# Compressed keys' products placed behind the first branch's second output products, and kept down-projection weights split one k-tile later, in a one-core decoder layer

## The chip, the cores and the metric

The kernel runs on one core of one Trainium2 chip. The metric is the device time of one execution in microseconds (us). TensorE (PE) does the matrix products, VectorE (DVE) and ScalarE (ACT) the element-wise work, GpSimd (POOL) a few small steps, and SyncE (SP) issues nearly all DMA transfers.

## The reference

One layer of a decoder on 256 positions with 2048 channels, in float32. Three token mixers share one input projection; a gated sum of their outputs goes through `w_o`, and a feed-forward block follows.

```
h = rms_norm(x);  p = h @ w_in
y_a = conformer_conv(...)            # GLU, causal conv of 31 taps, LayerNorm, silu, @ w_a_out
y_b = chunked_spatial_gating(...)    # gelu, LayerNorm, 128x128 mixing, @ w_b_out
y_c = native_sparse_attention(...)   # compressed, selected and window branch, @ w_c_out
x = x + rms_norm((g_a*y_a + g_b*y_b + g_c*y_c) @ w_o)
u = causal_depthwise_conv(rms_norm(x) @ w_up)
x = x + rms_norm((silu(u_g) * u_v) @ w_down)
```

The compressed branch joins 32 neighbouring positions of keys (and of values) to one block: `hid = silu(einsum(blocks + pe, w1))`, and `hid @ w2` gives the compressed key. These are the products that the first part of the change moves. The second part is in `@ w_down`.

## The kernel before

Float32 operands are multiplied as two reduced-precision parts. Every weight tile of 128 x 1024 is fetched by SP into a ring of five (`wraw`), ACT writes its high part (`whi`), DVE the rest (`wlo`), and PE takes three products (high by high, high by rest, rest by high; lines 194 to 197, 924 to 930). High and rest parts have rings of four tiles each, so a tile can only be split when PE is done with the tile four before it. One such matmul of 512 columns belongs to every line 195, 196, 197 or 929 in the profile.

**The middle of the kernel.** `branch(0, ...)` and `branch(1, ...)` (line 993) compute the gate of the gMLP and of the convolution branch (tiles `pg`) and their output products (tiles `py`), for four blocks of 512 channels each (`cb` 0 to 3). A gate block is 96 matmuls over 8 weight tiles, an output block 48 matmuls over 4 tiles in two halves (`q` 0 and 1). Between these, background work is issued from a queue of generators, `bg`. `pump(ns)` (line 91) adds a budget to `debt` and runs the generator at the head of the queue until the costs that it yields have used the budget up; a branch calls it with `BUDGET = BG` after the first three quarters of a gate block, behind the gate, between the two halves of an output block and behind it. `until(name)` empties the queue up to a mark.

In the queue stand, in this order when the branches begin: the rest of the convolution (`conv_gen`), its LayerNorm (`lna_gen`: mean product `lnpm`, squares, variance product `lnpv` on PE, `lnvar`, reciprocal root, and then eight rounds of normalization, tanh and conversion to `At`, lines 511 to 522), the spatial gating that is left, `cmp_prep(0)` (line 592: 16 additions of `pe` on DVE at line 601, four conversions `bk` on ACT and DVE at lines 605 and 606), `cmp_gen(0)` (line 609: four weight tiles `w1` split through the same rings, 32 products `zp`, two short products `hp` and `kcp`), the same two for the values, the compressed attention `cmp_attn` (line 705: scores `sc`, softmax `ce`, transposes `pcp` copied to `pct`), and the attention units (line 855). The text of the program gives only the order of issue and the dependencies; the framework's scheduler then fixes one order of instructions on each engine, and an engine does its instructions strictly in that order.

**The end.** The down-projection runs twice, over the first and the last 1024 channels: `first = Pair(0)`, `second = Pair(1)` (lines 1468 and 1478). Each has 24 plain k-tiles (`plain`, 12 matmuls, one weight tile) and ten pairs of k-tiles done with seven products in place of eight (`quad`, lines 939 to 959: 21 matmuls, two weight tiles `wraw` and `qa`, and on DVE four additions of 512 columns, three splits of 1024 and one of 512). In the second run the last six plain k-tiles are "kept": their weights are split ahead and multiplied only at the end, one 128 x 512 block of the result after the other, so that the closing norm of a block lies beside the products of the next (lines 1506 to 1526). Four of the six split tiles lie in space that the activations `gh` and `gl` have left, two in the rings. All splits of this part are issued in an order written by hand on ACT and DVE (`fixed`, line 888).

Of the kernel before, what the change touches and what calls it, by code (L numbers as in the profile page):

```python
# [24 lines left out]
R = mybir.dt.float32r  # L25
# [6 lines left out]
T = 256  # L32
# [6 lines left out]
PLAIN = [*range(22, 33), 21, 10, *range(33, NFT)]  # L39

NG, REST = 3, list(range(6, KT))
BA, BB, BC, BG = 2100, 2200, 2200, 5000
PR = 1000
NW0, _ = 9, 6
S1, S2, S3 = 6, 12, 14
# [11 lines left out]
def block(ctx: ExitStack, tc: tile.TileContext, x, xf, fp, cst, rows, sgw, w1, w2, wf_a, wt_bv, wf_bu, wf_c,  # L57
# [8 lines left out]
    marks = set()  # L66
# [21 lines left out]
    bg = deque()  # L88
# [296 lines left out]
    for k in range(KT):  # L385
        for j, cb in ((k, 0), (k, 1)) if k < 14 else ((14, 0), (15, 0)) if k == 15 else ():
            hi, lo = parts[j]
            c = slice(cb * 512, cb * 512 + 512)
# [203 lines left out]
    def cmp_prep(kv):  # L592
        bk = s8([128, 16, 2, 64], R, f"bk{kv}")
        bk_box[kv] = bk
        pe = fps[:, (C_PK, C_PV)[kv]:(C_PK, C_PV)[kv] + 16]
        for c in range(4):
            tmp = q1(f"bt{kv}{c}", (128, 4, 4, 16))
            G.memset(tmp[:, :, :, 15], 0.0)
            for i in range(4):
                jj = 4 * c + i  # L600
                V.tensor_scalar(tmp[:, i, :, 0:15], kd_t[:, kv, :, 2 * jj:2 * jj + 225:16], pe[:, jj:jj + 1], None,
                                op0=ALU.add)
                yield 150
            tf = tmp.rearrange("p i g n -> p i (g n)")
            S.activation(bk[:, 4 * c:4 * c + 4, 0], tf, AF.Copy)
            V.tensor_sub(bk[:, 4 * c:4 * c + 4, 1], tf, bk[:, 4 * c:4 * c + 4, 0].bitcast(F32))
            yield 350

    def cmp_gen(kv):
        bk = bk_box[kv]  # L610
        zp = bank([128, 2, 256], f"zp{kv}")
        for q in range(4):
            hi, lo = piece(w1[kv, :, q * 1024:q * 1024 + 1024], 1024)
            for i in range(4):
                jj = 4 * q + i
                st = bk[:, jj].rearrange("p a n -> p (a n)")
                PE.matmul(zp[:, 0], lhsT=st, rhs=hi[:, i * 256:i * 256 + 256], start=(jj == 0), stop=(jj == 15),
                          skip_group_check=True)
                PE.matmul(zp[:, 1], lhsT=st, rhs=lo[:, i * 256:i * 256 + 256], start=False, stop=(jj == 15),
                          skip_group_check=True)  # L620
            yield 1300
        zs = [q1(f"zs{kv}{a}") for a in range(2)]
        for a in range(2):
            S.activation(zs[a], zp[:, a], AF.Copy)
        hp = bank([128, 2, 64], f"hp{kv}")
        for h in range(2):
            for a in range(2):
                PE.matmul(hp[:, h], lhsT=zs[a][:, h * 128:h * 128 + 128], rhs=sel, start=(a == 0), stop=(a == 1))
        w2s = q1(f"w2s{kv}", (128, 2, 128))
        nc.sync.dma_start(w2s, w2[:, kv])  # L630
        hid = P1.tile([128, 2, 64], F32, tag="hid", bufs=2, name=f"hid{kv}")
        for h in range(2):
            th = P1.tile([128, 64], F32, tag="hth", bufs=2, name=f"hth{kv}{h}")
            S.activation(th, hp[:, h], AF.Tanh, scale=0.5)
            V.scalar_tensor_tensor(hid[:, h], th, 1.0, hp[:, h], op0=ALU.add, op1=ALU.mult)
            yield 200
        if kv == 0:
            ps = bank([128, 64], "kcp")
            for h in range(2):
                PE.matmul(ps, lhsT=w2s[:, h], rhs=hid[:, h],  # L640
                          start=(h == 0), stop=(h == 1))
            V.tensor_mul(kcb.rearrange("p g n -> p (g n)"), ps, cs[:, K_KM:K_KM + 64])
            yield 200
        else:
            hr = [q1(f"hidr{h}", (128, 2, 128)) for h in range(2)]
            for h in range(2):
                for gg in range(2):
                    V.tensor_copy(hr[h][:, gg].rearrange("p (j m) -> p j m", j=4),
                                  hid[:, h, gg * 32:gg * 32 + 32][:, None, :].to_broadcast([128, 4, 32]))
            yield 800  # L650
            for gg in range(2):
                ps = bank([128, 128], f"vcp{gg}")
                for h in range(2):
                    PE.matmul(ps, lhsT=hr[h][:, gg], rhs=w2s[:, h], start=(h == 0), stop=(h == 1))
                for j in range(4):
                    V.scalar_tensor_tensor(vbd[:, gg, j], ps, cs[:, K_RJ + j:K_RJ + j + 1], cs[:, K_BM:K_BM + 128],
                                           op0=ALU.mult, op1=ALU.mult)
                    yield 270

    sel = P1.tile([128, 64], F32, name="sel")  # L660
    with tc.issue_after(fetched[0]):
        V.tensor_add(sel, idn[:, 0:64], idn[:, 64:128])
    for kv in range(2):
        bg.append(cmp_prep(kv))
        bg.append(cmp_gen(kv))

    kkv = s8([128, 2, 1024], F32, "kkv")
# [325 lines left out]
    def branch(bi, act_of):  # L993

        for cb in range(4):
            pg = [PS.tile([128, 512], F32, tag="acc", name=f"pg{bi}{cb}{t}") for t in range(2)]
            for q in range(4):
                hs = granule(wt_g[(bi * 4 + cb) * 4 + q])
                for k in range(4 * q, 4 * q + 4):
                    hi, lo = hs[(k % 4) // 2]  # L1000
                    c = slice((k % 2) * 512, (k % 2) * 512 + 512)
                    for t in range(2):
                        ts = slice(t * 128, t * 128 + 128)
                        mm_t(pg[t], hT[:, k, 0, ts], hT[:, k, 1, ts], hi[:, c], lo[:, c], k == 0, k == KT - 1)
                if q < 3:
                    pump(BUDGET)
            tgs = {}
            for t in range(2):
                for a in range(2):
                    tgs[t, a] = q1(f"mg{bi}{cb}{t}{a}")  # L1010
                    with tc.high_priority(offset=int(PR)):
                        gated[0] = S.activation(tgs[t, a], pg[t][:, a * 256:a * 256 + 256], AF.Tanh,
                                                scale=rh[:, t:t + 1]).ins
            marks.add("gates")
            pump(BUDGET)
            py = [PS.tile([128, 512], F32, tag="acc", name=f"py{bi}{cb}{t}") for t in range(2)]
            for q in range(2):
                hs = granule(wt_p[(bi * 4 + cb) * 2 + q])
                if cb == 0 and q == 0:
                    until("BA"[bi])  # L1020
                act = act_of()
                for k in range(4 * q, 4 * q + 4):
                    hi, lo = hs[(k % 4) // 2]
                    c = slice((k % 2) * 512, (k % 2) * 512 + 512)
                    for t in range(2):
                        ts = slice(t * 128, t * 128 + 128)
                        pe_last[0] = mm_t(py[t], act[:, k, 0, ts], act[:, k, 1, ts], hi[:, c], lo[:, c], k == 0, k == 7)
                if q == 0:
                    pump(BUDGET)
            for t in range(2):  # L1030
                for a in range(2):
                    cc = slice(cb * 512 + a * 256, cb * 512 + a * 256 + 256)
                    y = mac[:, t, cc] if bi == 0 else tgs[t, a]
                    with tc.high_priority(offset=int(PR)):
                        V.scalar_tensor_tensor(y, tgs[t, a], 1.0, py[t][:, a * 256:a * 256 + 256], op0=ALU.add,
                                               op1=ALU.mult)
                        if bi:
                            V.tensor_add(mac[:, t, cc], mac[:, t, cc], y)
            pump(BUDGET)
# [436 lines left out]
        first.plain(i)  # L1476
    first.combine()
    second = Pair(1)
    kept = []
    i = 0  # L1480
    for j in range(NQ):
        while i < (3, 5, 7, 9, 10, 12, 14, 15, 17, 18)[j]:
            second.plain(i)
            if i == 2:
                for t in range(2):
                    for n in range(2):
                        first.result(t, n, fixed)
            i += 1
        second.quad(j)
        for x in range(0 if j < NQ - 5 else 1 if j < NQ - 1 else KEEP - 4):  # L1490
            k = NP - KEEP + len(kept)
            into = None
            if j < NQ - 1:
                kt = P2.tile([128, 11, T], R, tag=("gh", "gl")[j % 2], bufs=4, name=f"kept{k}")
                into = kt[:, 0:8].rearrange("p (a b) c -> p a (b c)", a=2)
            kept.append((PLAIN[k], weights(wt_dn[1, k], into)))
    assert i == NP - KEEP and len(kept) == KEEP
    nc.sync.dma_start(gain[:, 1024:2048], row(3072, 1024))
    back = s16(P0, [128, 2, D], F32, "back")
# [150 lines left out]
```

## Time and profile before

| | |
|---|---|
| time, median of 3 runs | 1594.03 us (1593.75 to 1594.13) |
| the profiled execution's own time | 1593.3 us |
| its span in the profile | 1591.5 us |
| mean granted TensorE clock | 0.993 |
| PE, DVE, ACT busy | 1559.4, 1291.6, 912.7 us |
| DMA | 193 GB/s mean |

The span is the time from the first to the last recorded instruction. A row of a timeline reads: start in us from the span's start, duration, engine, line of the kernel, operation, output <- inputs, number of instructions merged; in brackets the idle time of the engine before it and what ended it. A row of the view by windows gives for one stretch the busy time and number of instructions of PE, of PE's weight loads, DVE, ACT and POOL, then the granted TensorE clock (1.00 is full speed), the DMA share and GB/s.

### The profile page before, as it was taken

The numbers are of one execution on the slowest core, as the hardware profiler recorded it, in microseconds if no ns is written. First come the engines' busy times: TensorE is split into PE (matmuls) and PEld (weight loads), VectorE is DVE, ScalarE is ACT, GpSimd is POOL, SyncE is SP. The second block draws the span as 40 slices with busy tenths as digits, with TensorE's granted clock in tenths as the row PEclk, the third lists the DMA queues.
The fourth block names the chain that finished last, engine by engine and source line by source line (L and its number), as shares of the span: only waits on it lengthen the run. The fifth ranks groups of instructions, "written<-read, shape, count | busy, mean of one in ns | idle before, by whom it ended". The sixth has DMA issues, their size and how long they took to land.

```text
span 1591.5 us, 22436 instructions
## 1 busy us (share of the span) xinstructions
PE 1559.4 (98%) x8146; PEld 1323.1 (83%) x8146; DVE 1291.6 (81%) x2210; ACT 912.7 (57%) x1465; POOL 18.2 (1%) x46
## 2 busy tenths in 40 slices
PE   9999999995999999999999999999999999999997
PEld 7888899884887777888888888888888888888876
DVE  8899999778665654878886988888777777789898
ACT  7544544356486665556565765555555555566563
POOL 1000020000000000000000000000000000000000
PEclk9999999997999999999999999999999999999999
DMA  9555556654544445566674665556665656766672
GB/s 374 187 195 183 186 173 212 196 188 134 193 143 145 155 151 187 183 199 199 231 260 158 214 193 189 186 188 193 189 192 188 189 186 191 228 212 215 197 267 92
DMA packets 85440, 307.95 MB, mean 193 GB/s; under 512 B 9808, under 2 KB 10832, under 8 KB 84304
## 3 DMA queue, kind: packets, MB, share of 16 engines
q1 hardware_dynamic: 83952, 301.91, 58.1%
q0 software_dynamic: 944, 4.19, 0.8%
q8 instruction: 64, 1.05, 0.3%
q10 hardware_dynamic: 432, 0.41, 0.1%
q14 instruction: 48, 0.39, 0.1%
HBM read 301.23 MB, written 4.19 MB: 192 GB/s over the span
## 4 chain that ended last, share of the span: by engine, by line
PE 94%; DVE 3%; DMA 1%; ACT 1%; issue 1%; ACTq 0%; DVEq 0%
PE ps L175 29%; PE ps L182 15%; PE pd0b L929 5%; PE pg L195 4%; PE pg L197 4%; PE pg L196 4%; PE pd1a L929 3%; PE py L196 3%; PE py L197 3%; PE py L195 3%; PE poa L929 2%; PE pg1a L929 2%; PE pg0a L929 2%; PE pd0a L929 2%; PE po L195 1%; PE po L197 1%
## 5 line engine op out<-in xcount | busy, mean ns | idle before, releaser
L147 DVE TENSOR_TENSOR wlo<-wraw,whi 128x1024 fp32r<-128x1024 f32 (+1 forms) x376 | 457.4, 1218 | 108.4 <-ACT whi L146 102.0
L146 ACT ACTIVATE whi<-wraw 128x1024 fp32r<-128x1024 f32 (+1 forms) x376 | 393.3, 1052 | 156.4 <-PE pg L197 58.4
L175 PE MATMUL ps<-h2T,whi 128*128 128x512 f32 x1360 | 325.0, 391 | 0.0
L175 PEld LDWEIGHTS ps<-h2T,whi 128*128 128x128 f32 x1360 | 249.8, 188 | 48.2
L182 PEld LDWEIGHTS ps<-h2T,wlo 128*128 128x128 f32 x1360 | 174.5, 191 | 6.7
L182 PE MATMUL ps<-h2T,wlo 128*128 128x256 f32 x1360 | 176.6, 283 | 0.0
L175 PE MATMUL ps<-hT,whi 128*128 128x512 f32 x640 | 157.4, 392 | 0.0
L217 ACT ACTIVATE t<-ps 128x256 f32<-128x256 f32 x125 | 47.6, 382 | 187.0 <-PE ps L175 186.6
L894 DVE TENSOR_TENSOR wlowraw<-wraw,whiwraw 128x1024 fp32r<-128x1024 f32 x90 | 108.6, 1223 | 37.6 <-ACT whiwraw L894 36.1
L175 PEld LDWEIGHTS ps<-hT,whi 128*128 128x128 f32 x640 | 116.0, 188 | 21.3
L894 ACT ACTIVATE whiwraw<-wraw 128x1024 fp32r<-128x1024 f32 x90 | 94.6, 1057 | 48.6 <-PE py L197 17.4
L218 DVE TENSOR_TENSOR t<-ps,t 128x256 f32<-128x256 f32 x125 | 52.6, 422 | 70.3 <-ACT t L217 69.9
L478 DVE SCALAR_TENSOR_TENSOR cv<-hb,fps,cv 128x256 f32<-128x256 f32 x240 | 104.9, 477 | 0.2 <-ACT cv L474 0.2
L196 PE MATMUL pg<-wlo,hT 128*128 128x512 f32 x256 | 100.7, 394 | 0.0
L197 PE MATMUL pg<-whi,hT 128*128 128x512 f32 x256 | 100.7, 393 | 0.0
L195 PE MATMUL pg<-whi,hT 128*128 128x512 f32 x256 | 98.6, 393 | 0.0
L182 PEld LDWEIGHTS ps<-hT,wlo 128*128 128x128 f32 x640 | 84.7, 190 | 4.7
L182 PE MATMUL ps<-hT,wlo 128*128 128x256 f32 x640 | 86.8, 283 | 0.0
L196 PEld LDWEIGHTS pg<-wlo,hT 128*128 128x128 f32 x256 | 48.1, 188 | 10.8 <-issue 1.1
L197 PEld LDWEIGHTS pg<-whi,hT 128*128 128x128 f32 x256 | 48.1, 188 | 10.5 <-issue 0.7
L195 PEld LDWEIGHTS pg<-whi,hT 128*128 128x128 f32 x256 | 47.9, 188 | 10.4 <-issue 0.7
L1379 ACT ACTIVATE fa<-fs,fps 128x256 f32<-128x256 f32 x88 | 52.4, 596 | 1.2 <-DVE fs L220 0.9
(1334 smaller groups left out, 2792.3 us busy)
## 6 DMA issues: line engine op xcount, KB each, us to landing
wraw<-in_wf_up_dram SPq DMA_DIRECT2D x176, 512.0 KB, 4.1
wraw<-in_wt_g_dram SPq DMA_DIRECT2D x64, 512.0 KB, 3.8
wraw<-in_wt_p_dram SPq DMA_DIRECT2D x48, 512.0 KB, 4.3
wraw<-in_wt_dn_dram SPq DMA_DIRECT2D x48, 512.0 KB, 4.4
wraw<-in_wf_a_dram SPq DMA_DIRECT2D x32, 512.0 KB, 3.8
wraw<-in_wt_gp_dram SPq DMA_DIRECT2D x20, 512.0 KB, 4.3
wraw<-in_wt_dq_dram SPq DMA_DIRECT2D x20, 512.0 KB, 5.2
qa<-in_wt_dq_dram SPq DMA_DIRECT2D x20, 512.0 KB, 4.2
```

The costliest lines, as they stand in the source:

```text
L146: S.activation(hi[:, :n], raw[:, :n], AF.Copy)
L147: V.tensor_sub(lo[:, :n], raw[:, :n], hi[:, :n].bitcast(F32))
L175: ins = PE.matmul(ps[:, :, ts], lhsT=ws[k // 8][0][:, c:c + 128], rhs=mov[:, k, :, ts], start=(k == 0 and not t), stop=(k == n - 1), skip_ ...
L182: ins = PE.matmul(ps[:, 1, ts], lhsT=ws[k // 8][1][:, c:c + 128], rhs=mov[:, k, 0, ts], start=False, stop=False, skip_group_check=True).ins
L195: PE.matmul(ps, lhsT=xh, rhs=hi, start=first, stop=False)
L196: PE.matmul(ps, lhsT=xh, rhs=lo, start=False, stop=False)
L197: return PE.matmul(ps, lhsT=xl, rhs=hi, start=False, stop=last).ins
L218: V.tensor_add(t1 if rb is not None else dst, ps[:, 0], t1)
L478: V.scalar_tensor_tensor(ca[:, j], hb[:, j, k:k + T], w(j, k), ca[:, j], op0=ALU.mult, op1=ALU.add)
L894: seq[eng] = [op(*args, **kw).ins]
L929: ins = PE.matmul(bank, lhsT=a[x], rhs=w[y], start=first and j == 0, stop=last and j == 2).ins
L1379: S.activation(a, s, AF.Identity, bias=fps[:, C_FB + f:C_FB + f + 1], scale=w[2])
```

## The change

Three edits in the middle and one at the end:

- A generator `hold("outputs")` is put in the queue between `cmp_prep(0)` and `cmp_gen(0)`. As long as the mark "outputs" is missing it yields 6000 at each step, so that a `pump` gets no further.
- `branch` sets the mark at `cb == 1`, `q == 0`, ahead of the pump between the two halves of the second output block.
- The budget `BG` of a pump in the branches rises from 5000 to 6500.
- In the second run of the down-projection a kept tile is no longer fetched and split directly behind quads 5 to 8 but behind the first plain k-tile that follows each of them; and the space it lies in alternates by the tile's number and no longer by the quad's.

```diff
-BA, BB, BC, BG = 2100, 2200, 2200, 5000
+BA, BB, BC, BG = 2100, 2200, 2200, 6500
...
+    def hold(name):
+
+        while name not in marks:
+            yield 6000
+
     for kv in range(2):
         bg.append(cmp_prep(kv))
+        if kv == 0:
+            bg.append(hold("outputs"))
         bg.append(cmp_gen(kv))
...
                 if q == 0:
+                    if cb == 1:
+                        marks.add("outputs")
                     pump(BUDGET)
...
-    kept = []
+    kept, keep = [], 0
+
+    def keep_more(n, into):
+
+        for _ in range(n):
+            k = NP - KEEP + len(kept)
+            dst = None
+            if into:
+                kt = P2.tile([128, 11, T], R, tag=("gh", "gl")[k % 2], bufs=4, name=f"kept{k}")
+                dst = kt[:, 0:8].rearrange("p (a b) c -> p a (b c)", a=2)
+            kept.append((PLAIN[k], weights(wt_dn[1, k], dst)))
+
     i = 0
     for j in range(NQ):
         while i < (3, 5, 7, 9, 10, 12, 14, 15, 17, 18)[j]:
...
             i += 1
+            keep_more(keep, True)
+            keep = 0
         second.quad(j)
-        for x in range(0 if j < NQ - 5 else 1 if j < NQ - 1 else KEEP - 4):
-            k = NP - KEEP + len(kept)
-            into = None
-            if j < NQ - 1:
-                kt = P2.tile([128, 11, T], R, tag=("gh", "gl")[j % 2], bufs=4, name=f"kept{k}")
-                into = kt[:, 0:8].rearrange("p (a b) c -> p a (b c)", a=2)
-            kept.append((PLAIN[k], weights(wt_dn[1, k], into)))
+        keep = 1 if j >= NQ - 5 else 0
+    keep_more(KEEP - len(kept), False)
```

In the built program the order of instructions on the engines changes as follows. On PE the variance product `lnpv` stands behind 14 matmuls of the second gate block (behind 70 of them before); the first `zp` stands behind the first 24 matmuls of the second output block (ahead of all of them before); the short products `hp` and the transposes move with them; `pcp` of the second half of the positions stands 15 matmuls behind its scores `sc` (39 before). From the attention units of the second half of the positions to the end of the branches PE's order is the same, with the last attention matmul 69 places ahead of the first product of the next stage in both. In the last 60 us the four kept splits each change places with the plain split that follows them, on ACT and on DVE; SP's order of transfers there is the same but for which of the two weights comes first.

## The prediction

> **What bounds the kernel now.** I read the page's busy times first, then PE's waits, then the stretches around the longest wait, then the end.
>
> ```profile
> span 1591.5 us, 22436 instructions
> PE 1559.4 (98%) x8146; PEld 1323.1 (83%) x8146; DVE 1291.6 (81%) x2210; ACT 912.7 (57%) x1465; POOL 18.2 (1%) x46
> ```
>
> PE works for 98% of the span; 32 us are left, some 9 of them at the very end. The view of PE's waits names what ended the others:
>
> ```profile
> engine line waited for: us in total, times, longest us
> PE zp L617 <- DVE bk L606: 16.8, 1, 16.8
> PE py L196 <- DVE wlo L147: 1.5, 1, 1.5
> ...
> PE s L751 <- ACT pct L738: 1.2, 1, 1.2
> PE pd1a L929 <- DVE wlowraw L894: 1.2, 2, 0.6
> PE py L195 <- ACT whi L146: 0.4, 1, 0.4
> ```
>
> One wait of 16.8 us makes up half: the compressed keys' first product waits for its operand `bk`. The others are a tenth of it. So the change can win at most what stands around this wait, and lose wherever the moved work is late elsewhere. The timelines around it, of PE, DVE and ACT:
>
> ```profile
> 350.72 0.60 PE L485 MATMUL lnpv<-lnv,ones 128*128 128x256 f32 x2
> 351.35 0.42 DVE L506 TENSOR_SCALAR lnvar<-lnpv 128x256 f32<-128x256 f32 x1 [0.39 <-PE lnpv L485]
> 356.84 0.39 PE L197 MATMUL pg<-whi,hT 128*128 128x512 f32 x1
> 360.23 0.60 ACT L515 ACTIVATE lz<-cv,fps 128x256 f32<-128x256 f32 x1 [1.91 <-DVE cv L514]
> 372.18 0.43 ACT L605 ACTIVATE bk<-bt 128x256 fp32r<-128x256 f32 x1
> 374.04 0.58 PE L617 MATMUL zp<-whi,bk 128*128 128x256 f32 x1 [16.81 <-DVE bk L606]
> ```
>
> The chain is: variance product, `lnvar`, root, normalization (L515 is its first ACT step at 360.23), then ACT's conversion of `bk` at 372.18, `zp` at 374.04. PE is idle from 357.23. In that time the clock also falls:
>
> ```profile
> 359.50:360.50 1.00, 0.00 (x0) 0.00 (x0) 1.00 (x4) 0.27 (x1) 0.00 (x0) 0.69 0.44 176
> 376.50:377.00 0.50, 0.50 (x5) 0.50 (x4) 0.00 (x0) 0.49 (x1) 0.00 (x0) 0.54 0.00 0
> 374.00:377.00 3.00, 2.96 (x14) 2.97 (x15) 1.32 (x4) 1.21 (x2) 0.50 (x4) 0.51 0.00 0
> ```
>
> A mean of 0.69 over 359.50 to 360.50 with states of 1 and 0.5 puts the fall at 359.88, 2.65 us after PE stopped; 0.54 over the third half microsecond puts the rise at 376.96, 2.92 us after it went on. So a long wait costs half of these 2.92 us more, or a little less, as 14 products were done: some 1.3 us.
>
> **The change, part by part.**
>
> *Where PE now meets `zp`.* 24 matmuls of the second output block come first. One takes
>
> ```profile
> 1565.25 17.01 PE pd1a L929 x75
> ```
>
> 17.01 / 75 = 0.227 us, so PE comes free at 357.23 + 24 x 0.227 = 362.7. Nothing ahead of it on PE is added.
>
> *When `bk` is ready.* The product `lnpv` stands 70 - 14 = 56 matmuls earlier: 56 x 0.227 = 12.7 us, so `lnvar` starts at 351.35 - 12.7 = 338.6 (its squares have nothing else to wait for: the mean product `lnpm` moves ahead of the whole first output block). From `lnvar` to the first L515 is the same work with the same three splits between: 360.23 - 351.35 = 8.9 us, so 347.5. From there to the conversion of `bk` ACT took 372.18 - 360.23 = 12.0 us before, without one weight split between, as PE stood still. In the new order five splits stand between them, since PE goes on. A split costs ACT and DVE:
>
> ```profile
> 377.41 2.96 ACT L146 ACTIVATE whi<-wraw 128x1024 fp32r<-128x1024 f32 x3 [0.42 <-PE zp L617]
> 1546.60 2.35 DVE L894 TENSOR_TENSOR wlowraw<-wraw,whiwraw 128x1024 fp32r<-128x1024 f32 x2
> 1550.20 1.22 DVE L894 TENSOR_TENSOR wloq_3b<-wraw,whiq_3b 128x1024 fp32r<-128x1024 f32 x1
> 372.79 1.37 ACT L605 ACTIVATE bk<-bt 128x256 fp32r<-128x256 f32 x3
> ```
>
> On DVE 2.35 - 1.22 = 1.13 us; on ACT (2.96 - 1.06) / 2 = 0.95 us, with 1.06 for one split (the row at 436.31 further below). Five make 4.8 us: `bk`'s conversion on ACT at 347.5 + 12.0 + 4.8 = 364.3. From there to `zp` it was 374.04 - 372.18 = 1.9 us; one DVE split now stands between, so 3.0: `zp` goes at 367.3. The wait is 367.3 - 362.7 = 4.6 us in place of 16.8: **12.2 us won**. Bounds: one split more or less on the way, 11.1 to 13.4. The conversions of the other three quarters (1.37 us for three on ACT) come before PE needs them, as each quarter feeds eight products of 0.12 us or, at half speed, 0.21. The half-speed loss behind this wait stays, since 4.6 is above 2.65.
>
> *The small waits behind `zp`.* Before, the second half of the output block waited 0.4 + 1.5 us for splits that stood behind the preparation of the values on DVE. These splits now come early, and the waiting place becomes the next gate block's first tile, whose split has the same preparation ahead of it. Bounds 0 and 1.9 won; I take 1.4, nearer to the full, because PE meets it after 24 matmuls more.
>
> *A new wait at the transposes.* Each transposition `pcp` waits for a softmax on DVE that needs its scores `sc` first:
>
> ```profile
> 425.40 1.87 PE L709 MATMUL sc<-kcb,qf 128*128 128x32 f32 x16
> 427.31 0.43 DVE L720 TENSOR_TENSOR ce<-sc,cs 128x256 f32<-128x256 f32 x1 [1.60 <-PE sc L709]
> 433.31 0.42 DVE L732 TENSOR_TENSOR ce<-ce,cm 128x256 f32<-128x256 f32 x1
> 436.07 0.38 PE L736 MATMUL pcp<-idn,ce 128*128 128x128 f32 x2
> 436.31 1.06 ACT L146 ACTIVATE whi<-wraw 128x1024 fp32r<-128x1024 f32 x1 [1.66 <-PE py L197]
> 437.28 0.36 ACT L738 ACTIVATE pct<-pcp 128x256 f32<-128x256 f32 x1
> 437.70 1.16 PE L751 MATMUL s<-kkv,qf 64*128 64x128 f32 x16 [1.25 <-ACT pct L738]
> ```
>
> From the end of `sc` (427.27) to the end of L732 (433.73) are 6.5 us; 39 matmuls (8.9 us) covered them. Now 15 are left, 3.4 us: PE waits 6.5 - 3.4 = 3.1 us with the gate block's last tiles and the first attention scores queued behind it. **3.1 us lost**, bounds 2 and 4 (one split on the way). Whether the clock falls too is open: 3.1 is just 0.45 above the one fall that the trace shows. Bounds 0 and 1.3; I take 0.6, the middle. The Trainium skill, "TensorE: Matmul & The Clock Gate", section "What's actually happening", says that the gate closes after a whole idle window of about 3.4 us whose phase is free of the kernel; the trace's fall and rise lie 376.96 - 359.88 = 17.08 us apart, five times that, which agrees; but the fall came 2.65 us into the wait, so the window that closed the gate had held work, which does not. What the rule makes of the time is a rival below.
>
> *The attention's first product.* `pct` waited behind a split on ACT (436.31 to 437.28). With PE waiting, ACT has nothing ahead of `pct`, so of the 1.25 us there remain the 437.70 - 437.28 = 0.42 from the copy's start to `s`: 0.8 won, bounds 0 and 0.8.
>
> *The kept tiles.* The sums of DVE and ACT work and of the transfers are unchanged; four pairs of splits change places.
>
> ```profile
> 1508.01 1.23 DVE L894 TENSOR_TENSOR wlowraw<-wraw,whiwraw 128x1024 fp32r<-128x1024 f32 x1 [1.07 <-ACT whiwraw L894]
> 1529.94 0.69 DVE L894 TENSOR_TENSOR fin<-wraw,qa 128x512 f32<-128x512 f32 x1 [1.60 <-DMA wraw<-in_wt_dq_dram]
> 1530.00:1571.00 41.00, 39.71 (x171) 31.27 (x170) 40.80 (x48) 23.96 (x26) 0.00 (x0) 1.00 0.50 166
> 1547.87 0.50 PE L929 MATMUL pd1a<-wlowraw,gh 128*128 128x512 f32 x1 [0.62 <-DVE wlowraw L894]
> ```
>
> A plain split needs a ring place and so can wait for PE (1.07 us at 1508.01); a kept split of these four needs none and filled such a hole. Behind quad 5 the plain one now comes first and may wait that 1.07 us, but DVE stood 1.60 us before quad 6's transfer anyway (1529.94), which covers it. From there DVE is full (40.80 of 41 us) up to the last block, in either order, so the last quad's parts are ready when they were; the 0.62 us that PE waited for a plain tile goes, to come back in front of the next quad. I take 0, from 0.6 won to 1.0 lost; without the transfer's cover it is the 1.0.
>
> *Sum* against the profiled execution: 12.2 + 1.4 - 3.1 - 0.6 + 0.8 + 0 = 10.7 us, span 1591.5 - 10.7 = 1580.8. With the 1.8 us that lie around the span (1593.3 of its own time) 1582.6; the median of the runs stood 0.7 above that execution, so 1594.03 - 10.7 = **1583.3**.
>
> **The rivals.**
>
> *No fall of the clock behind the short waits.* Fall and rise before lie 376.96 - 359.88 = 17.08 us apart, five times 3.42. If the clock is set in stretches of that length, and a wait must fill one of them whole, 3.1 us can't make it fall and 4.6 us only at some phases: 0.6 to 0.6 + 1.3 us more won, 1582.7 to 1581.4. For it: the 17.08 us; against: 2.65 us were enough. This is also what the rule of the Trainium skill named above ("TensorE: Matmul & The Clock Gate", "What's actually happening") would make of it.
>
> *The tail loses.* DVE, full for the last 41 us, has no place to catch up: if quad 6's transfer lands earlier than in this execution, the ring wait of 1.07 us is not covered, and the end comes 1.0 later: 1584.3.
>
> *The keys come no earlier.* If the earlier variance product is eaten by the splits that now share ACT and DVE, `bk` is ready at 374.0 as before and only the cover of 24 matmuls (5.4 us) is won: 5.4 + 1.4 - 3.1 - 0.6 + 0.8 = 3.9, 1590.1. The change then does what it says, but the wait is only shortened by what stands before it. Against it: the three parts of the chain add up to 7 us less, with the splits counted.
>
> *Slower: the attention comes late.* The hold stops the queue, and all attention work stands behind it. If that chain ends later than the branches, PE idles before the next stage:
>
> ```profile
> 626.14 1.94 PE L751 MATMUL O<-ep,kkv 128*64 128x512 f32 x8
> 642.92 0.39 PE L929 MATMUL pg0a<-whiwraw,hT 128*128 128x512 f32 x1
> 440.00:640.00 200.00, 200.00 (x988) 155.15 (x987) 111.21 (x272) 132.55 (x304) 0.57 (x1) 1.00 0.50 157
> ```
>
> Cover is 642.92 - 628.08 = 14.8 us; the whole gain is gone when the chain is 14.8 + 10.7 = 25.5 us later, and at 30 us the time is 1583.3 + 15.2 = 1598.5. Against it: in the new order the last attention product stands as far ahead of the next stage as before, and DVE (111 of 200 us) and ACT (133) have room to catch up.
>
> **How the numbers follow.** Forecast 0.62, no fall 0.20, tail 0.08, keys no earlier 0.07, attention late 0.03. The range 1581.3 to 1586.3 holds the first three: below by the whole gain of the second, above by 3 us, which is about what the bounds of `zp` (1.1), of `pcp` (0.9), of the clock (0.7) and of the small waits (1.4) add up to when not all go wrong at once. A measurement of this kernel tells 0.2% (3.2 us) from no change. The first three and most of the fourth are faster by more than that: 0.93; within it 0.04; slower 0.03.
>
> **What would show it.** `zp`'s wait on `bk` between 3.5 and 5.7 us; a new wait of about 3 us of `pcp` on L732's `ce`; `s` on `pct` near 0.4; `lnvar` near 338.6, first L515 near 347.5; no wait over 1 us in the last 60 us; the attention's last product some 11 us earlier, at the same distance from the next stage. I am wrong if `zp` waits over 8 us, if a wait appears between 440 and 640 us, or if the time lies above 1590.

## The result, and the profile after

| | before | after |
|---|---|---|
| time, median of 5 runs each | 1593.94 us (1593.75 to 1594.13) | 1583.40 us (1582.03 to 1584.43) |
| ratio, 95% interval | | 0.9933 (0.9918 to 0.9947) |
| span of the profiled execution | 1591.5 us | 1582.7 us |
| its own time | 1593.3 us | 1584.43 us |

The change made the kernel faster by 10.5 us in the medians, where 10.7 had been forecast (1583.3). The profiled executions lie 8.8 us apart in their spans (8.8 by the terms weighed further below): the one of after was the slowest of its five. The terms are weighed against the spans, as the prediction made them against a span.

The changed kernel's page has these busy times:

```profile
span 1582.7 us, 22435 instructions
PE 1562.7 (99%) x8146; PEld 1325.7 (84%) x8146; DVE 1291.0 (82%) x2210; ACT 911.7 (58%) x1465; POOL 18.2 (1%) x46
```

Its view of PE's waits (us in total, times, longest) has these lines:

```profile
PE zp L617 <- DVE bk L606: 4.0, 1, 4.0
PE pcp L743 <- DVE ce L739: 3.0, 1, 3.0
...
PE s L758 <- ACT pct L745: 0.5, 1, 0.5
PE pv L401 <- ACT swraw L117: 0.5, 1, 0.5
PE pg L196 <- DVE wlo L147: 0.2, 1, 0.2
PE pd1a L936 <- DVE wloq_4b L901: 0.2, 1, 0.2
```

The wait of 16.8 us has become 4.0; a wait of 3.0 stands at the transposes. (Lines behind the new code have numbers 7 higher: L743 is what was L736.) The timeline shows the milestones that the prediction named:

```profile
339.03 0.42 DVE L506 TENSOR_SCALAR lnvar<-lnpv 128x256 f32<-128x256 f32 x1 [1.30 <-PE lnpv L485]
347.77 0.59 ACT L515 ACTIVATE lz<-cv,fps 128x256 f32<-128x256 f32 x1
364.06 0.72 ACT L605 ACTIVATE bk<-bt 128x256 fp32r<-128x256 f32 x2
367.08 0.58 PE L617 MATMUL zp<-whi,bk 128*128 128x256 f32 x1 [4.04 <-DVE bk L606]
425.65 0.69 PE L743 MATMUL pcp<-idn,ce 128*128 128x128 f32 x2 [3.00 <-DVE ce L739]
426.81 2.08 PE L758 MATMUL s<-kkv,qf 64*128 64x128 f32 x16 [0.47 <-ACT pct L745]
617.58 1.94 PE L758 MATMUL O<-ep,kkv 128*64 128x512 f32 x8
634.36 0.39 PE L936 MATMUL pg0a<-whiwraw,hT 128*128 128x512 f32 x1
```

`lnvar` starts at 339.03 (forecast 338.6), the normalization at 347.77 (347.5), the conversion of `bk` at 364.06 (364.3), `zp` at 367.08 (367.3). The last attention product comes 8.6 us earlier than before, and so does the next stage. So the whole difference arises ahead of 440 us, and the clock is where sum and profile part. The windows of the changed kernel, cut at the places where its clock changes (columns as before: PE, weight loads, DVE, ACT, POOL, granted clock):

```profile
360.29:363.70 3.41, 2.75 (x13) 1.94 (x11) 3.41 (x13) 3.41 (x9) 0.00 (x0) 1.00 0.77 238
363.70:367.11 3.41, 0.03 (x1) 0.03 (x1) 3.41 (x13) 2.94 (x8) 0.03 (x1) 1.00 0.14 56
367.11:370.52 3.41, 3.41 (x16) 3.41 (x17) 2.84 (x6) 1.06 (x1) 0.47 (x4) 0.50 0.73 199
...
421.72:425.13 3.41, 0.93 (x5) 0.43 (x3) 3.04 (x7) 1.06 (x1) 0.00 (x0) 1.00 0.41 133
425.13:428.55 3.42, 2.42 (x18) 2.03 (x18) 2.50 (x9) 1.84 (x5) 0.00 (x0) 0.50 0.57 174
428.55:431.96 3.41, 3.41 (x18) 3.19 (x17) 3.41 (x22) 0.83 (x2) 0.00 (x0) 0.50 0.00 0
```

In the middle the clock fell twice. At `zp` it stayed at half for one stretch of 3.41 us, full of work: 3.41 / 2 = 1.7 us lost. At `pcp` it stayed there for two, 6.83 us with 2.42 + 3.41 = 5.83 us of work: 2.9 us lost. Before, the one fall held 2.92 us of work, 1.5 lost.

### The profile page after: what moved, and what is told of

It reads as the page before. It is cut to its first block, busy times and chain, and to the rows that moved or that the text cites. A ratio compares the mean times of both kernels' runs of the same rounds, so it can differ in the third digit from the quotient of the medians.

```text
span 1582.7 us, 22435 instructions
## 1 busy us (share of the span) xinstructions
PE 1562.7 (99%) x8146; PEld 1325.7 (84%) x8146; DVE 1291.0 (82%) x2210; ACT 911.7 (58%) x1465; POOL 18.2 (1%) x46
## 4 chain that ended last, share of the span: by engine, by line
PE 94%; DVE 3%; ACT 1%; issue 1%; DMA 0%; DVEq 0%; SPq 0%; ACTq 0%
PE ps L175 29%; PE ps L182 15%; PE pd0b L936 5%; PE pd1a L936 4%; PE pg L196 3%; PE pg L197 3%; PE pg L195 3%; PE py L196 3%; PE py L195 3%; PE py L197 2%; PE poa L936 2%; PE pg1a L936 2%; PE pg0a L936 2%; PE pd0a L936 2%; PE pd1b L936 1%; PE po L197 1%
```

## The experiments

Each kernel was timed in five rounds (4, 5 or 11 times in all) against the kernel before on the same chip; the four of a group shared chip and runs of before (medians 1592.73, 1592.66 and 1593.19 us), so small differences are read within a group. The expectations are written on the scale of the first measurement (1593.94 us before); where a microsecond matters, the gain over the group's own kernel before is compared with the gain expected. Each kernel has one profile, and its terms are those of that execution.

### Each edit alone, and the change without the last

**Budget alone.**

```diff
-BA, BB, BC, BG = 2100, 2200, 2200, 5000
+BA, BB, BC, BG = 2100, 2200, 2200, 6500
```

> The kernel before with the budget of 6500 alone, without the hold and the kept tiles' new order. My theory: the budget moves the whole queue forward, and PE meets zp earlier too: it now stands 35 matmuls behind lnpv, inside the second gate block. From the end of lnpv to zp the chain takes 367.08 - 338.9 = 28 us in the changed kernel and 23 us in the one before; 35 matmuls cover 35 x 0.227 = 8 of them. PE waits 15 to 17 us in all, at zp or ahead of it, as it did before: 1592 to 1595 us. Rival: the earlier variance product is what brings the gain, whatever PE meets first: 12.7 us earlier less 4.8 us of splits, 7.9 us, so 1586.

Measured: 1593.47 us (1591.21 to 1594.35), ratio 1.0002 (0.9993 to 1.001). No gain; the rival's 1586 is out. But the waits were not the 15 to 17 us of my expectation in full. Its view of PE's waits:

```profile
PE zp L617 <- DVE bk L606: 7.0, 1, 7.0
PE pg L195 <- ACT whi L146: 3.5, 2, 2.3
PE kcp L640 <- DVE hid L635: 2.6, 1, 2.6
...
PE pg L196 <- DVE wlo L147: 1.2, 2, 0.6
```

And its windows, cut where the clock may change:

```profile
340.96:344.37 3.41, 1.58 (x6) 0.67 (x6) 3.26 (x4) 1.14 (x2) 0.00 (x0) 1.00 0.63 178
344.37:347.78 3.41, 3.41 (x10) 2.51 (x8) 3.34 (x10) 2.10 (x3) 0.00 (x0) 0.50 0.48 156
347.78:351.20 3.42, 1.06 (x4) 0.30 (x2) 1.84 (x4) 3.39 (x8) 0.00 (x0) 1.00 0.00 0
351.20:354.61 3.41, 2.94 (x7) 2.37 (x8) 3.07 (x9) 3.41 (x11) 0.51 (x4) 0.50 0.50 149
354.61:358.02 3.41, 0.97 (x4) 0.46 (x3) 1.81 (x4) 2.85 (x6) 0.00 (x0) 1.00 0.01 5
358.02:361.43 3.41, 0.00 (x0) 0.00 (x0) 3.41 (x18) 2.00 (x6) 0.43 (x3) 0.50 0.49 154
361.43:364.85 3.42, 2.31 (x11) 2.31 (x12) 2.40 (x9) 1.01 (x3) 0.19 (x1) 0.50 0.00 0
364.85:368.26 3.41, 3.41 (x18) 3.41 (x18) 2.25 (x2) 2.11 (x3) 0.00 (x0) 0.50 0.17 25
...
378.50:381.91 3.41, 3.41 (x18) 3.41 (x18) 0.80 (x1) 1.23 (x2) 0.00 (x0) 0.50 0.58 181
```

The waits come to 7.0 + 3.5 + 2.6 + 1.2 = 14.3 us, down from 16.8 + 1.5 + 0.4 + 1.2 = 19.9. But cut into pieces they made the clock fall four times (the last time behind a stretch with 0.85 us of work), and the rows at 0.50 hold 3.41 + 2.94 + 2.31 + 3.41 + 3.41 = 15.5 us of work, 7.7 us lost in place of 1.5. What the waits gave, 5.6 us, the clock took, 6.2.

**Hold alone**, with the budget left at 5000 (the kernel before, plus `hold`, its place in the queue and its mark).

> The kernel before with the hold alone, the budget left at 5000. My theory: zp stands 48 matmuls further back, behind the whole output block (48 x 0.227 = 10.9 us of cover), while bk is ready later than 374.0 by the splits that PE's going on lets through, some five of 1.1 us: a wait of 16.8 - 10.9 + 5.5 = 11.4 us, 5.4 won; the small waits of the output block (1.9) go too, and the scores stay far ahead of the transposes, so no wait of pcp: 7.3 us won, 1586.6, with one fall of the clock. Rival: the hold wins by cover alone and bk comes when it did: a wait of 5.9 us, 10.9 + 1.9 won, 1581. Second rival: all of the gain hangs on the budget, 1594.

Measured: 1583.85 us (1582.75 to 1584.55), ratio 0.9944 (0.993 to 0.9957). Its `zp` in the timeline:

```profile
379.26 0.58 PE L617 MATMUL zp<-whi,bk 128*128 128x256 f32 x1 [11.01 <-DVE bk L606]
```

And the window in which its clock was at half:

```profile
372.82:383.05 10.23, 3.79 (x17) 3.79 (x18) 8.53 (x32) 5.80 (x15) 0.57 (x4) 0.50 0.17 51
```

The wait is the 11 us of my theory (11.4), with `bk` 5.2 us later than before, so the first rival (a wait of 5.9) is out. Against its group's kernel before it gained 1592.73 - 1583.85 = 8.9 us, 1.6 more than the 7.3 of the theory. Some of that I had left out: with `zp` later, the 1.2 us of `s` on `pct` and half of the pd1a waits are gone from its list too. The second rival is out: the hold without the budget has the changed kernel's time.

**Kept tiles alone** (the last part of the diff on the kernel before).

> The kernel before with the kept tiles' new order alone. My theory: no more than the 0.6 us wait of pd1a either way, 1593.3 to 1594.6, and the 16.8 us wait as before. Rival: the tail loses the 1.07 us of a ring wait: 1595.0.

Measured: 1593.58 us (1592.72 to 1595.01), ratio 1.0006 (0.9997 to 1.0015). No gain, and a loss of 1 us or even 2 is not excluded by it; the last group below comes back to this.

**Budget and hold**, the kept tiles in the old order.

> The changed kernel with the kept tiles in the old order. My theory: the same as the changed kernel within 0.7 us, 1582.7 to 1584.1, with waits of 4.0 us at zp and 3.0 us at pcp, and a wait of 0.6 us of pd1a at the end that the changed kernel has not. Rival: the kept tiles' order is worth 1 us or costs it: 1584.5 or 1582.3. Both: times spread over 2 us from run to run like the changed kernel's (1582.0 to 1584.4), if that spread comes from where the falls of the clock lie in the two short waits.

Measured: 1582.91 us (1582.82 to 1583.54), ratio 0.9939 (0.9927 to 0.9952), with waits of 4.0 and 3.0 us and two falls of the clock as in the changed kernel. The spread was 0.7 us and not 2: the falls are there, the spread isn't, so that part of the expectation missed. By the medians of this group the budget is worth 1583.85 - 1582.91 = 0.9 us on top of the hold, though it shortens `zp`'s wait by 7 us; but the times of the two overlap, and their profiled spans (1581.2 and 1581.8 us) differ the other way, so no gain of the budget is shown. Most of the 7 us is paid back at the transposes (3.0 + 0.5 us of waits that the hold alone has not) and in the clock: here 2.86 and 5.54 us of work at half speed,

```profile
366.60:370.01 3.41, 2.86 (x13) 2.87 (x14) 2.97 (x7) 1.07 (x2) 0.50 (x4) 0.50 0.58 168
424.63:431.46 6.83, 5.54 (x31) 4.92 (x32) 5.91 (x29) 2.68 (x7) 0.00 (x0) 0.50 0.30 99
```

4.2 us lost against 3.79 / 2 = 1.9. By these terms 7.0 - 3.5 - 2.3 = 1.2 us would be left.

### The two waits and the clock

**Filler ahead of the transposes.**

```diff
         pp = bank([128, 2, 128], f"pcp{qt}")
+        ppf = pp.rearrange("p a n -> p (a n)")
+        if qt == 1:
+            in_turns([(ppf, hT[:, 0, 0, 0:128], hT[:, 0, 0], True, True)] * 20)
```

> The changed kernel with 20 idle products of 256 columns (0.12 us each, 2.4 us in all) ahead of the 15 matmuls that stand in front of pcp; they write the bank that pcp overwrites, and nothing uses them. They take PE's wait of 3.0 us without making pcp later, as this waits for DVE. Theory: the clock's fall at 425.13 cost 2.9 us (6.3 us of work at half speed); with 0.6 us of idle time left it doesn't come: 1583.4 - 2.9 = 1580.5. Rival: the time is that of the wait alone, the clock's fall costs PE nothing that counts: 1583.4. Second rival: the products delay pcp by their 2.4 us: 1585.8 or, without the fall, 1583.

Measured: 1581.51 us (1581.04 to 1582.56), ratio 0.9928 (0.9916 to 0.9941). The clock stayed at 1.00 there, and `pcp` no longer waits. But `s` now waits 1.2 us for `pct`, and the fall behind `zp` lasted two stretches in this execution (4.89 us of work at half speed), so the time by itself tells too little: it is 1592.66 - 1581.51 = 11.2 us below its group's kernel before, where the theory has 13.4 and the rival 10.5. The last group repeats it beside the changed kernel.

**The mark one half block later.**

```diff
                 if q == 0:
-                    if cb == 1:
-                        marks.add("outputs")
                     pump(BUDGET)
+                elif cb == 1:
+                    marks.add("outputs")
```

> The changed kernel with the mark set behind the second half of the output block, so that zp stands behind all 48 matmuls of it. Theory: 24 matmuls more are 5.4 us of cover for a wait of 4.0: it goes, with its fall of the clock (1.7 us), apart from pieces below 1 us; pcp now stands directly behind its scores, with no split between on DVE: 6.4 - 2 x 1.2 = 4.0 us of waiting in place of 3.0. 1583.4 - 4.0 - 1.7 + 1.0 = 1578.7, up to 1580 with the pieces. Rival: bk comes later by the splits that 24 matmuls more let through (two, 2.2 us), so 2 us of the wait and the fall stay: 1582 to 1583.

Measured: 1581.71 us (1581.06 to 1583.69), ratio 0.9931 (0.9918 to 0.9943). `zp`'s wait on `bk` is gone, with its fall of the clock, as the theory has it; in its list of waits stand

```profile
PE pcp L743 <- DVE ce L739: 4.3, 1, 4.3
...
PE zp L619 <- DVE wlo L147: 1.0, 2, 0.8
PE pg L196 <- DVE wlo L147: 0.6, 1, 0.6
PE s L758 <- ACT pct L745: 0.5, 1, 0.5
```

Nearly half of the gain of 5.7 us was spent again: 1.3 at `pcp`, 1.4 in pieces on weight splits. Its span, 1580.0, is 2.7 below that of the changed kernel's first profile. The times show less: 11.0 us below its group's kernel before, where the changed kernel had 10.5 and has 9.3 in the last group, so by them alone a gain is not clear; the theory's 13.9 to 15.2 did not come. The gain is the size of the rival's (10.9 to 11.9), but not its cause: `zp` does not wait for `bk`.

**The transposes one pump later.**

```diff
         V.tensor_mul(e, e, bi(m))
-        yield 1300
+        yield 5000
```

> The changed kernel with a cost of 5000 in place of 1300 ahead of the transposes pcp, so that they are issued one pump later, 57 rows behind their scores in place of 18. Theory: the wait of 3.0 us, the 0.5 us of s on pct and the fall of the clock (2.9) go: 1583.4 - 6.4 = 1577.0; zp's wait of 4.0 stays. Rival: the attention behind it comes later by a pump and PE waits for it between 440 and 640 us: 1580 or more. Second rival: the fall of the clock costs nothing: 1579.9.

Measured: 1578.03 us (1577.29 to 1578.37), ratio 0.9905 (0.9891 to 0.9918). The waits of `pcp` and `s` are gone and nothing comes instead; the attention behind is not waited for. It is 1592.66 - 1578.03 = 14.6 us below its group's kernel before, where the theory has 16.9 and the second rival 14.0, so the time alone doesn't tell these two apart; the fillers below do. Its span, 1576.7, is 6.0 below the changed kernel's, where 6.4 was expected. What it lost of that stands at `zp`, where this execution spent

```profile
365.85:372.68 6.83, 5.30 (x25) 5.30 (x26) 5.79 (x10) 3.20 (x6) 0.51 (x4) 0.50 0.52 157
```

two stretches, 2.65 us lost in place of 1.7, at a wait of nearly the same length (4.1 us).

**Both.**

> Both: the mark behind the second half of the output block and the cost of 5000 ahead of pcp. Theory: both waits and both falls of the clock go, some small waits of 2 us in all come instead: 1583.4 - 4.0 - 1.7 - 6.4 + 2 = 1573.3. Rival: the work held back twice is late at the attention: 1577 or more. If the spread of the changed kernel's times (2.4 us) comes from the falls of the clock, these times lie within 0.6 us of each other.

Measured: 1574.80 us (1574.61 to 1575.12), ratio 0.9885 (0.987 to 0.99). The clock stays at 1.00 throughout the middle; no wait above 1 us is left but one of 1.4 at the kernel's start. It beats both kernels. Its span, 1573.4, is 9.3 us below the changed kernel's, where the theory has 10.1; against its group's kernel before it gained 17.9 us, where the theory has 20.6 and the rival 16.9. What is missing was not traced further, but PE waits for no attention work, so it isn't the rival's cause. The times lie within 0.5 us of each other, as expected if the spread came from the falls. Whether this version needs the budget of 6500 was not run.

### On one chip: the clock, and the kept tiles

**The changed kernel again.**

> The changed kernel once more, beside the next three on the same chip. Its profile is to show the same waits (4.0 at zp, 3.0 at pcp) and a fall of the clock at each, of a whole number of stretches of 3.41 us. Theory: the stretches don't start with the kernel, so what the falls cost differs from one execution to the next: in the first profile 1.7 and 2.9 us. 1583 us, with a spread of 1 us or more. Rival: the falls cost the same in each execution, and the spread has another source.

Measured: 1583.85 us (1583.38 to 1584.41), ratio 0.9942 (0.993 to 0.9955). Its waits are again 4.0 us at `zp` and 3.0 at `pcp`, and the falls of one and two stretches (rows below) cost 1.5 and 2.8 us, where the first profile has 1.7 and 2.9.

**Fillers in both waits**: the filler above, and 28 such products chained behind the last matmul of the output block's half, into `zp`'s bank.

```diff
         zp = bank([128, 2, 256], f"zp{kv}")
+        if kv == 0:
+            last = pe_last[0]
+            for _ in range(28):
+                with tc.issue_after(last):
+                    last = PE.matmul(zp[:, 0], lhsT=hT[:, 0, 0, 0:128], rhs=hT[:, 0, 0], start=True, stop=True,
+                                     skip_group_check=True).ins
```

> The changed kernel with idle products in both waits: the 20 ahead of pcp as in the filler above, and 28 of 256 columns (3.4 us) directly ahead of the first zp, into its own bank; nothing uses what they write. Waiting for DVE stays 4.0 and 3.0 us, but PE has 0.6 us of each left without work. Theory: no fall of the clock in the middle of the kernel; the changed kernel's time less 4 us (1.5 to 1.7 at zp, 2.5 to 2.9 at pcp), and a smaller spread. Rival: the falls of the clock cost little that counts, so it is within 1 us of the changed kernel's time.

Measured: 1580.60 us (1580.16 to 1581.16), ratio 0.9922 (0.991 to 0.9935): 3.25 us below the changed kernel beside it, and all five times lie below all five of that. First the changed kernel's two stretches at half speed and its middle, then the middle of the one with fillers:

```profile
366.52:369.93 3.41, 2.99 (x14) 2.99 (x15) 2.84 (x7) 1.06 (x1) 0.50 (x4) 0.50 0.68 177
424.55:431.38 6.83, 5.62 (x31) 5.00 (x32) 5.90 (x29) 2.68 (x7) 0.00 (x0) 0.50 0.29 92
360.00:440.00 80.00, 72.15 (x388) 61.14 (x387) 62.80 (x171) 43.65 (x89) 0.50 (x4) 0.94 0.55 175
```

```profile
360.00:440.00 80.00, 77.61 (x452) 66.48 (x451) 64.83 (x176) 44.78 (x90) 0.50 (x4) 1.00 0.56 181
```

The waits left in the one with fillers, beside that at the start:

```profile
PE s L767 <- ACT pct L754: 1.2, 1, 1.2
PE zp L623 <- DVE bk L606: 0.7, 1, 0.7
```

The falls cost (2.99 + 5.62) / 2 = 4.3 us; without them, and with 0.7 us more of `s` waiting for `pct`, 3.6 are to be won, and the spans differ by 1582.2 - 1578.7 = 3.5. Work that nobody uses made the kernel faster by holding the clock up. The spread stayed at 1.0 us in both, and in all five executions with fillers the mean granted clock was 0.998 or 0.999, so the falls are not its only source. They may be one: of the 21 executions of the kernel before in the first group, the ten with a mean clock of 0.993 took 1591.86 to 1592.73 us, the eleven with 0.992 took 1592.41 to 1594.66. The other source was not looked for.

**Both late, kept tiles in the old order**, and **both late again**.

> The version with the late mark and the late transposes, with the kept tiles in the old order. It has no wait above 1 us left, so it tells what the kept tiles' new order is worth by itself, against the next run on the same chip. Theory: the two orders are within 0.5 us: from the first product of the last run of the down-projection to the end, the profiles so far show 124.3 to 124.7 us for the new order and 123.5 to 125.0 for the old. Rival: the old order is faster by the 1 us that 123.5 and 124.7 differ by. 1574 to 1575 us.

> The version with the late mark and the late transposes, with the kept tiles in the new order, once more: 1574.8 us, spread 0.6 us. Against the run before it tells the worth of the kept tiles' order: theory 0 with 0.5 either way, rival 1 us slower than the old order.

Measured: old order 1573.99 us (1573.65 to 1575.98), ratio 0.9883 (0.987 to 0.9897); new order 1574.45 (1574.24 to 1574.69), ratio 0.9884 (0.9869 to 0.9899). What the kept tiles' order does shows from the first product of the last run of the down-projection to the end of the span. In the old order it starts, in the kernel before, in the hold alone and in the old order of this group (span 1574.3), at

```profile
1466.55 0.39 PE L929 MATMUL pd1a<-whiwraw,gh 128*128 128x512 f32 x1
```

```profile
1457.65 0.39 PE L936 MATMUL pd1a<-whiwraw,gh 128*128 128x512 f32 x1
```

```profile
1448.15 0.39 PE L936 MATMUL pd1a<-whiwraw,gh 128*128 128x512 f32 x1
```

and in the new order, in the changed kernel and in the second of this pair (span 1572.5), at

```profile
1457.98 0.39 PE L936 MATMUL pd1a<-whiwraw,gh 128*128 128x512 f32 x1
```

```profile
1447.81 0.39 PE L936 MATMUL pd1a<-whiwraw,gh 128*128 128x512 f32 x1
```

So the old order takes 1591.5 - 1466.55 = 125.0, 1581.2 - 1457.65 = 123.6 and 1574.3 - 1448.15 = 126.2 us, the new one 1582.7 - 1457.98 = 124.7 and 1572.5 - 1447.81 = 124.7. The profiled execution of the old order here was its slowest (1575.98); the three others lie at 1573.65 to 1574.19, below all four of the new order. Over all profiles the new order takes 124.3 to 124.8 us (nine of them), the old one 123.5 to 126.2 (five): the new order is steady, the old one at times better by 1.1 us and at times worse by 1.5, and the new one has no gain in the median. The medians differ by 0.46, and the times of the old order overlap those of the new, so theory and rival (0.5 and 1 us) are not told apart.

## Why the prediction was right, and where it was not

The terms, in the profiled executions (gain positive):

| term | forecast | measured | from |
|---|---|---|---|
| `zp` on `bk` | 12.2 | 12.8 | 16.81 - 4.04 |
| small weight waits behind it | 1.4 | 1.7 | 1.5 + 0.4 - 0.2 |
| `pcp` on `ce` | -3.1 | -3.0 | new wait |
| clock | -0.6 | -3.2 | 2.92 / 2 - (3.41 + 5.83) / 2 |
| `s` on `pct` | 0.8 | 0.8 | 1.25 - 0.47 |
| tail | 0 | 0.2 | 125.0 - 124.7 |
| `pv` on `swraw`, near the start | - | -0.5 | not in the list of before |
| sum | 10.7 | 8.8 | spans: 8.8 |

- **The chain to `bk`** held at every milestone to half a microsecond: the variance product earlier, the five splits that PE's going on lets through, the cover of 24 matmuls. "Keys no earlier" fell: `zp` stands at 367.08 and not at 374.
- **The wait at the transposes** came where and as long as forecast (3.00 us, forecast 3.1).
- **The clock is the term that was mis-sized**, and its bounds failed with it. The prediction gave the second fall "Bounds 0 and 1.3; I take 0.6, the middle", from the one fall of before, as if the rise always came some 2.9 us after PE goes on. It cost 2.9 us: PE waited 0.52 us ahead of `pcp` and another 0.47 between `pcp` and `s` in the first stretch at half speed, which held 2.42 of 3.41 us of work, and the clock rose only after the next. The fall behind `zp`, taken as unchanged, went from 1.5 to 1.7.
- **No fall behind the short waits**, with a chance of 0.20, fell: both waits made the clock fall, in each of three profiles of this order.
- **The tail** lost nothing; the loss of 1.07 us that was feared did not come. The 0.6 us waits of `pd1a` on `wlowraw` did go, and with the order: the old order shows 0.5 to 1.2 us of them in each of five profiles, the new one none in nine, and at most 0.2 us of `pd1a` on `wloq_4b`. But the stretch to the end is no shorter for it in general (see the last group), and what takes the gain back was not traced.
- **The attention** was not late: its last product and the next stage both moved by 8.6 us, at the same distance.
- The median agrees with the forecast better than the terms do: 10.5 us there, 8.8 between the profiled executions, 1593.19 - 1583.85 = 9.3 in the last group. In the profiles the mis-sized clock, 2.6 us, is offset by 0.6 + 0.3 + 0.1 + 0.2 us of other terms, with the 0.5 of `pv` against, which leaves 1.9; the rest of the agreement comes from which executions were profiled. That the median hit the forecast to 0.2 us is luck; the terms support it to about 2.
- **What the prediction did not see**: that the hold alone would do. It took the earlier variance product, which is the budget's work, as the larger part of the 12.2 us. With 5000 the scheduler puts `zp` behind 48 matmuls in place of 24, and the time is within 1 us of both edits together; most of the budget's 7 us at `zp` go into the transposes' wait and the clock.

## What to carry to other kernels

When background work is pulled forward in an order that an engine follows strictly, look at the shortest distance between a product and the product that needs its result through another engine: here the budget moved 7 us from one such place to the next, where a transpose held back by one number won some 5 us (a ratio of 0.9905, against 0.9933 and 0.9942 of the changed kernel) and the whole budget no more than 0.9, which the runs don't tell from nothing. Count a wait of PE not by its length but with the clock behind it: short waits can cost as much as the long one that they replace, and idle products (48 here) in a wait that can't be removed pay for themselves. Measure each edit of a change alone; of these three one had the gain.

## What the runs showed of the hardware

The clock was set in stretches of 3.41 us: every stay at half speed in the middle of the kernel is a whole number of them, in these profiles 1, 2, 3, 5 or 6. What decides is the work in the stretch that has just ended, and the stretch need not be empty. It fell after stretches with 0.03, 0.75, 0.93, 0.97, 1.06 and 1.58 us of work, and not after 2.05 (near the end of the kernel with the budget alone), 2.16 (behind the filler) or more. The 0.75 and the 2.92 are the kernel before's, by its windows; the row after them is the one with 2.05:

```profile
356.47:359.88 3.41, 0.75 (x4) 0.29 (x2) 3.34 (x6) 1.06 (x1) 0.00 (x0) 1.00 0.44 159
373.54:376.96 3.42, 2.92 (x13) 2.93 (x14) 1.78 (x6) 1.60 (x3) 0.50 (x4) 0.50 0.01 2
```

```profile
1579.99:1583.41 3.42, 2.05 (x10) 1.36 (x8) 2.28 (x6) 1.23 (x4) 0.00 (x0) 1.00 0.41 157
```

It rose after 2.86, 2.92, 2.94, 2.99 and 3.41 us, and not after 2.31 or 2.42. So the bound for a fall lies somewhere between 1.58 and 2.05 us of 3.41, and for a rise between 2.42 and 2.86; all 14 profiles agree. The stretches don't start with the kernel: in two profiles of the changed kernel one ended 0.03 us behind the start of `zp` (367.11 and 367.08) and 0.42 ahead of it (366.52 and 366.94). So the same wait at `zp`, 4.0 or 4.1 us, cost one stretch and 1.4 to 1.7 us in three profiles, and two stretches and 2.4 to 2.7 us in two. The Trainium skill, "TensorE: Matmul & The Clock Gate", section "What's actually happening", has a stretch of 3413 ns that runs free of the kernel, which these profiles bear out, and a fall after an idle window, which they do not: 1.58 us of work was not enough to keep the clock. By that rule the wait of 3.0 us at `pcp` would have cost nothing more; it cost 2.9.
